# Output projection by seven half-size products, the second half of the tokens tile by tile

## The chip, the cores and the metric

The kernel runs on one core of one Trainium2 chip. The metric is the device time of one execution in microseconds (us). The engines are TensorE (PE in the profile; PEld is its weight load), VectorE (DVE), ScalarE (ACT), GpSimd (POOL) and SyncE (SP), whose queue here only starts DMA transfers.

## The reference, cut to what matters

The input is 1024 tokens of 1024 features in float32. Two attention branches with 512 features each, `y_a` and `y_b`, are merged by gates, projected and added to the input; a SwiGLU feed-forward block follows.

```python
def mixer_block(h, ...):
    proj = h @ w_in                       # 1024 x 4352
    ...
    merged = sigmoid(ga) * (y_a @ w_ba) + sigmoid(gb) * (y_b @ w_bb)    # 1024 x 1024
    return merged @ w_o                   # the output projection, 1024 x 1024 x 1024

h = h + mixer_block(rms_norm(h, norm_mix), ...)
h = h + (silu(hn @ w_gate) * (hn @ w_up)) @ w_down      # hn = rms_norm(h, norm_ffn), 2816 wide
out = rms_norm(h, norm_final)
```

## The kernel before, in words

Every float32 operand of a large product is split in two parts that TensorE takes at full rate: ScalarE writes the high part (line 112), and VectorE or GpSimd subtracts it from the source for the low part (line 113). `split(hi, lo, src, engine)` is this pair; its last argument says who does the subtraction. A product then takes three matmuls for each 128x128 block of weights and 512 columns: high by high, high by low, low by high. Twelve matmuls of 128x512 are a contraction over 512, and are called one step below.

The stages on TensorE, with the start of each in the profiled execution:

- Projections, the windowed attention and the differential attention, with the gate products as filler (to 635.9 us).
- The branch products (`ppa`, line 551, from 635.9). First `y_b @ w_bb`, then `y_a @ w_ba`: 16 steps each, one for every block of 128 features (o) and half of the tokens. For each step VectorE multiplies the sigmoid gate by the PSUM bank (lines 833 and 854). For the second branch GpSimd then adds the first branch's part, which waits in `tb` (line 855), and the sum is split into `mT` (line 856, subtraction on VectorE). The second branch's weight splits (`wbha`) have their subtraction on GpSimd. In the second half of this stage `prep_wo` splits the first blocks of `w_o`, on GpSimd too.
- The output projection (`po`, line 882, from 725.6). For each column half q and group of four token tiles, eight contraction blocks c are accumulated in four PSUM banks; the last column half of the last four tiles goes tile by tile. That is 2 x 8 x 8 x 3 = 384 matmuls. VectorE adds the banks to the input `h2` (`out_add`, line 887). As each token tile is complete, `norm_f` normalises it (ScalarE square, GpSimd root, VectorE scaling, line 1017), and `turn_f` transposes it on TensorE, eight transposes a tile (`ptn_f`, line 1031), into the blocks `b11`, `b21`, `b22` of the feed-forward block's right side, and into the sums of blocks that its products need.
- The gate and up products (`pg`, line 1116, from 818.9). They already go by seven half-size products instead of eight (Strassen's method in Winograd's form): for each of 11 pairs of feature blocks (fp) and both weights (i), products 1, 2, 6, 5, 7, 3, 4 are one step each. Products 1 and 2 need only the blocks themselves; 6, 5, 7 and 4 need sums of token blocks (`t_ops`, split by `split_t`) and sums of weight blocks (lines 940 to 946, on VectorE). The order starts with products 1 and 2 of the first `N_EARLY = 3` pairs, twelve steps that give the other engines time to make the sums.
- The down product (`pd`, line 1210, from 1240.9), by seven products too, and the final normalisation.

PSUM has eight banks of 128x512. Operands live in rings: eight `op` tiles of split weights, five `raw` tiles of loaded ones; a tile is written again when its last reader is done. From the branch products on, the order of TensorE's instructions is the order in which the code writes them; up to the down product, the order on the other engines and on SP's queue is fixed when the program is built, by a planner that simulates the whole. In the chip's queues every instruction waits in place, so what stands behind a waiting instruction on its engine waits too.

```python
    def split(hi, lo, src, lo_eng):                                # lines 111 to 113
        nc.scalar.activation(hi, src, AF.Copy)
        lo_eng.tensor_tensor(lo, src, f32(hi), ALU.subtract)
    ...
        nc.vector.tensor_tensor(gt, gt, ps, ALU.mult)              # lines 854 to 858
        nc.gpsimd.tensor_tensor(gt, gt, tb[:, o, tk], ALU.add)
        split(mT[:, o, 0, tk], mT[:, o, 1, tk], gt, nc.vector)
        if n >= 8:
            prep_wo(0, n - 8)
    ...
        for n, (a, b) in enumerate(((0, 0), (0, 1), (1, 0))):      # lines 881 to 883
            nc.tensor.matmul(ps, mT[:, c, a, t * P:(t + 1) * P], wos[q, c][:, b],
                             start=(c == 0 and n == 0), stop=(c == DC - 1 and n == 2))
```

## Time and profile before

| | us |
|---|---|
| median of 3 runs (lowest, highest) | 1462.27 (1459.82, 1462.70) |
| the profiled execution | 1461.45 |
| its span, first to last instruction | 1459.6 |
| TensorE busy in the span | 1441.7 |
| VectorE, ScalarE, GpSimd busy | 856.9, 660.8, 522.4 |

The span is 1.85 us shorter than the profiled execution's own time; what lies around it is not in the trace. All durations below are from that one execution. The granted TensorE clock is full in it but for the start and the end.

### The profile page before, as it was taken

The page shows a single profiled execution, that of the slowest core. Times are in us where ns is not written, and L with a number is a line of the kernel's source. Part 1 is how long each engine was busy: PE and PEld are TensorE (multiplying, and loading weights), DVE is VectorE, ACT ScalarE, POOL GpSimd, SP SyncE. Part 2 cuts the span into 40 slices and gives each one's busy share as a digit, 9 for nine tenths or more (in the row PEclk, how much of TensorE's full clock was granted, in tenths as well). Part 3 has the DMA queues.
Part 4 walks back from the last instruction along what each step waited for, and adds up shares of the span by engine and source line. Part 5 has one row for each costly group of instructions (what it writes and reads, how often), then busy time and mean ns, then how long its engine had stood idle before and what let it go on. Part 6 is the DMA issues. An engine that isn't in the chain of part 4 may idle for free.

```text
span 1459.6 us, 21074 instructions
## 1 busy us (share of the span) xinstructions
PE 1441.7 (99%) x7375; PEld 1237.3 (85%) x7375; DVE 856.9 (59%) x1680; ACT 660.8 (45%) x1247; POOL 522.4 (36%) x496
## 2 busy tenths in 40 slices
PE   8999999999999999999999999999999999999997
PEld 7998989988898989888788878888888888788886
DVE  6456326528686868433514876555555553787667
ACT  6356336525455555444515643333333333444454
POOL 4143223313323232224834246454444542000444
PEclk9999999999999999999999999999999999999999
DMA  7334453372524251086523534333333333954443
GB/s 238 88 100 114 116 130 90 77 223 84 146 74 145 74 153 66 30 280 205 188 99 128 160 96 152 123 104 99 100 102 109 102 101 102 348 189 140 123 128 139
DMA packets 157241, 192.06 MB, mean 132 GB/s; under 512 B 16256, under 2 KB 101696, under 8 KB 157136
## 3 DMA queue, kind: packets, MB, share of 16 engines
q1 hardware_dynamic: 157136, 190.73, 41.7%
q8 instruction: 58, 0.95, 0.3%
q14 instruction: 47, 0.39, 0.1%
HBM read 130.19 MB, written 53.94 MB: 126 GB/s over the span
## 4 chain that ended last, share of the span: by engine, by line
PE 85%; POOL 4%; issue 4%; DMA 3%; DVE 1%; ACT 1%; SPq 0%; POOLq 0%; ACTq 0%; DVEq 0%
PE pg L1116 28%; PE pp_g L200 11%; PE pd L1210 8%; PE po L882 6%; PE aps L607 4%; PE pp_qb L200 3%; PE pp_va L200 3%; PE pp_ka L200 3%; PE apy L649 3%; PE pp_qa L200 3%; POOL oa L113 3%; PE apt L636 2%; PE ppa L551 2%; PE bpt L338 2%; PE bpy L344 2%
## 5 line engine op out<-in xcount | busy, mean ns | idle before, releaser
L1116 PE MATMUL pg<-t,wop 128*128 128x512 f32 x1056 | 243.1, 389 | 1.6 <-DVE wop L113 1.6
L1116 PEld LDWEIGHTS pg<-t,wop 128*128 128x128 f32 x1056 | 198.1, 188 | 43.3 <-DVE wop L113 2.0
L113 POOL TENSOR_TENSOR wop<-wf,wop 128x512 fp32r<-128x512 f32 x118 | 157.7, 1338 | 156.8 <-ACT wop L112 144.4
L1210 PE MATMUL pd<-ob,oa 128*128 128x512 f32 x924 | 210.2, 389 | 1.6 <-DVE ob L113 1.2
L1210 PEld LDWEIGHTS pd<-ob,oa 128*128 128x128 f32 x924 | 173.3, 188 | 38.5 <-DVE ob L113 1.6
L1116 PE MATMUL pg<-b,wop 128*128 128x512 f32 x792 | 183.2, 389 | 0.0
L1116 PEld LDWEIGHTS pg<-b,wop 128*128 128x128 f32 x792 | 148.5, 188 | 30.7
L113 POOL TENSOR_TENSOR wl_c<-w_c,wh_c 128x1024 fp32r<-128x1024 f32 x32 | 77.6, 2426 | 162.5 <-ACT wh_c L112 130.6
L112 ACT ACTIVATE wop<-wf 128x512 fp32r<-128x512 f32 x128 | 80.2, 631 | 81.9 <-PE pg L1116 50.8
L618 ACT ACTIVATE as<-as,amn 128x1040 f32<-128x1040 f32 x64 | 74.5, 1164 | 73.9 <-DVE amn L613 73.6
L113 POOL TENSOR_TENSOR oa<-ra,oa 128x512 fp32r<-128x512 f32 x33 | 44.0, 1335 | 171.6 <-ACT oa L112 170.2
L200 PE MATMUL pp_g<-hT_hi,wh_c 128*128 128x512 f32 x256 | 101.3, 396 | 0.0
L200 PE MATMUL pp_g<-hT_hi,wl_c 128*128 128x512 f32 x256 | 100.9, 394 | 0.0
L200 PE MATMUL pp_g<-hT_lo,wh_c 128*128 128x512 f32 x256 | 100.9, 394 | 0.0
L112 ACT ACTIVATE oa<-ra 128x512 fp32r<-128x512 f32 x77 | 48.7, 632 | 106.9 <-PE pd L1210 51.8
L607 PE MATMUL aps<-ak,aq 128*128 128x352 f32 (+1 forms) x384 | 92.9, 326 | 0.7 <-DMA ak<-ka_d 0.7
L882 PE MATMUL po<-woh,mT 128*128 128x512 f32 x384 | 88.6, 390 | 0.0
L940 DVE TENSOR_TENSOR s<-wf,wf 128x512 f32<-128x512 f32 x22 | 26.1, 1190 | 105.7 <-DMA wf<-in_w_ff_gate_dram 49.4
L882 PEld LDWEIGHTS po<-woh,mT 128*128 128x128 f32 x384 | 71.7, 188 | 14.7
L607 PEld LDWEIGHTS aps<-ak,aq 128*128 128x128 f32 x384 | 69.6, 188 | 15.1 <-DMA ak<-ka_d 1.0
L613 DVE CUSTOM_DVE_ANT_0 as<-aps,dist,amn 128x352 f32<-128x352 f32 (+1 forms) x128 | 71.3, 563 | 10.1 <-PE aps L607 8.1
L325 POOL TENSOR_SCALAR bs<-bs,bdn 128x432 f32<-128x432 f32 (+1 forms) x64 | 37.0, 596 | 86.9 <-DVE bdn L323 64.7
(258 smaller groups left out, 2951.8 us busy)
## 6 DMA issues: line engine op xcount, KB each, us to landing
ra<-aop SPq DMA_DIRECT2D x77, 256.0 KB, 2.6
w_c<-in_w_in_dram SPq DMA_DIRECT2D x33, 512.0 KB, 4.1
wf<-in_w_ff_gate_dram SPq DMA_DIRECT2D x24, 512.0 KB, 3.8
wf<-in_w_ff_up_dram SPq DMA_DIRECT2D x24, 512.0 KB, 3.8
aop<-as SPq DMA_DIRECT2D x44, 256.0 KB, 2.1
aop<-c SPq DMA_DIRECT2D x33, 256.0 KB, 2.0
g_d<-gate_stage SPq DMA_DIRECT2D x32, 256.0 KB, 2.0
gt<-g_d SPq DMA_DIRECT2D x32, 256.0 KB, 3.4
```

What stands on the lines that cost most here:

```text
L112: nc.scalar.activation(hi, src, AF.Copy)
L113: lo_eng.tensor_tensor(lo, src, f32(hi), ALU.subtract)
L200: nc.tensor.matmul(ps[:, :n], a[:, c, :], b[:, c, at:at + n], start=(c == 0 and i == 0), stop=(c == DC - 1 and i == 2))
L325: nc.gpsimd.tensor_scalar(st[:, r, :W], st[:, r, :W], dn[:, r:r + 1], 1.0, ALU.mult, ALU.mult)
L338: nc.tensor.transpose(pt[:kp, r, :], st[:, r, o:o + P] if k < 8 else md[:, r], ident)
L607: nc.tensor.matmul(ps[:, :n], qs[m][:, t * P:(t + 1) * P], ks[m][:, vv, k0:k0 + n], start=(vv == 0), stop=(vv == 1))
L613: nc.vector.tensor_tensor_reduce(s[m][:, a:b], ps[:, a - k0:b - k0], far_by, slope, low, ALU.add, ALU.min, mn[:, m, i + j:i + j + 1])
L618: nc.scalar.activation(s[m][:, 0:L], s[m][:, 0:L], AF.Exp, bias=low, scale=-1.0, accum_out=dn[:, m:m + 1])
L649: nc.tensor.matmul(py[:, cols], v[:kp, a, k, :], at_[:kp, k, b, :], start=(k == 0 and j == 0), stop=(k == 8))
L882: nc.tensor.matmul(ps, mT[:, c, a, t * P:(t + 1) * P], wos[q, c][:, b], start=(c == 0 and n == 0), stop=(c == DC - 1 and n == 2))
L1116: nc.tensor.matmul(ps, op[:, x, c, :], b[:, y, c, :], start=(p in (1, 2, 5) and c == 0 and n == 0), stop=(p in (4, 2, 3) and c == 3 and n ...
L1210: nc.tensor.matmul(ps[u], oa[:, a, u * P:(u + 1) * P], ob[:, b, :], start=(p in (1, 2, 5) and j == 0 and k == 0), stop=(p in (2, 3, 4) and ...
```

## The change

The output projection, too, goes by seven half-size products. The merged tensor is kept as float32 in four blocks, by half of the features (contraction) and half of the tokens: `a11`, `a12` (first half of the tokens), `a21`, `a22` (second half); `w_o` is loaded in four blocks `w11`, `w21`, `w12`, `w22`. Sums of each are made by VectorE, and by GpSimd for `a21 - a11` and for `w21`. Products 1, 2, 6, 5, 3 are done in steps by contraction block j, for four token tiles u at once; products 7 and 4, which only the second half of the tokens needs, tile by tile (`product_t`), with the transposes of finished tiles between them. `out_add` is called for the banks of every product. `m2` takes the place of `ya0`, the first half of `y_a`; `ahead` makes the splits of the step eight steps later. With this go smaller edits:

- the splits of `w_ba` have their subtraction on VectorE instead of GpSimd; `mT` and its splits are gone, and products 1 and 2 have their eight splits of each side made during the branch products;
- in the feed-forward block products 1 and 2 of a fourth pair come ahead of the sums (`N_EARLY = 4`, 16 steps). The first three pairs keep their product 1 in a PSUM bank as before; the fourth's is copied to SBUF, and ScalarE copies it back into a bank before product 6 adds to it;
- the weight sums of the first pair go to GpSimd; the splits of the token sums are spread over steps 2 to 11; the tiles' transposes come one later.

```diff
-WB_BUFS = 5
+WB_BUFS = 7
-P_BUFS = 7
+P_BUFS = 10
...
+    a21, a22 = (keep.tile([P, 4, 512], F32, name=f"m_{n}") for n in ("21", "22"))
+    m0, m1, ya0 = block_pair(0, "m0", F32), block_pair(1, "m1", F32), block_pair(2, "ya0", F32R)
+    a11, asum, a12, w11 = m0[:, 0], m0[:, 1], m1[:, 0], m1[:, 1]
...
+    def right_o(p, j):
...
+        split(ob[:, 0], ob[:, 1], src, nc.vector)
+    def left_o(p, j):
+        oa = lefts[p, j] = op_tile(f"oa_o{p}_{j}")
+        split(oa[:, 0], oa[:, 1], {1: a11, 2: a12, 6: a11, 5: asum, 3: a12}[p][:, j], nc.gpsimd)
...
+    order_a = [(o, 0) for o in range(6)] + [(0, 1), (6, 0), (1, 1), (7, 0)] + [(o, 1) for o in range(2, DC)]
     for n, (o, half) in enumerate(order_a):
         if o not in ws_a:
-            ws_a[o] = branch_w(ypool, o, w_ba, "a")
+            ws_a[o] = branch_w(ypool, o, w_ba, "a", None, nc.vector)
         gt, ps, tk = gated(1, o, half, ws_a[o], ya)
         nc.vector.tensor_tensor(gt, gt, ps, ALU.mult)
-        nc.gpsimd.tensor_tensor(gt, gt, tb[:, o, tk], ALU.add)
-        split(mT[:, o, 0, tk], mT[:, o, 1, tk], gt, nc.vector)
-        if n >= 8:
-            prep_wo(0, n - 8)
+        nc.gpsimd.tensor_tensor(merged(o, half), gt, merged(o, half), ALU.add)
+        if n < 4:
+            right_o(1, n)
+        elif n < 8:
+            right_o(2, n - 4)
+            left_o(1, n - 4)
+        elif n < 12:
+            if n > 9:
+                left_o(2, n - 10)
+        elif n < 14:
+            left_o(2, n - 10)
+            if n == 12:
+                m2 = block_pair(2, "m2", F32)
+                w22, w12 = m2[:, 0], m2[:, 1]
+                load_wo(w12, 0, 1)
+                load_wo(w22, 1, 1)
...
+    for j in range(4):
+        tt_v(asum[:, j], a21[:, j], a22[:, j], ALU.add)
+        tt_p(a21[:, j], a11[:, j], a21[:, j], ALU.subtract)
+        tt_v(a11[:, j], asum[:, j], a11[:, j], ALU.subtract)
+        tt_v(w11[:, j], w12[:, j], w11[:, j], ALU.subtract)
+        tt_v(t2[j // 2][:, j % 2 * 512:j % 2 * 512 + 512], w22[:, j], w11[:, j], ALU.subtract)
+    steps_o = [(p, j) for p in (1, 2, 6, 5, 3) for j in range(4)]
...
+    for n, (p, j) in enumerate(steps_o):
...
+        for u in range(4):
+            for k in (2, 3) if last else (j,):
+                product_o(p, k, u)
+            if j == 3:
+                out_add(u + 4 * (p == 5), int(p > 2), sets_o[p][u])
+                if p == 3:
+                    norm_f(u)
+        for k in (n - 1, n) if last else (n,):
+            ahead(k)
+            if k < 4:
+                tt_v(a12[:, k], a12[:, k], a11[:, k], ALU.subtract)
+            elif k < 8:
+                tt_p(w21[:, k - 4], w21[:, k - 4], t2[(k - 4) // 2][:, k % 2 * 512:k % 2 * 512 + 512], ALU.subtract)
+            elif k < 12:
+                tt_v(w12[:, k - 8], w22[:, k - 8], w12[:, k - 8], ALU.subtract)
+    TURN_O = {1: 0, 2: 1, 3: 2, 4: 3, 6: 4}
+    for n, (p, u) in enumerate(((7, 0), (7, 1), (4, 0), (4, 1), (7, 2), (7, 3), (4, 2), (4, 3))):
+        product_t(p, u)
+        out_add(4 + u, int(p == 7), set1[u])
+        if p == 4:
+            norm_f(4 + u)
+        if n in TURN_O:
+            turn_f(TURN_O[n])
...
-    N_EARLY = 3
+    N_EARLY, N_KEPT = 4, 3
-        tt = nc.vector.tensor_tensor
+        tt = nc.vector.tensor_tensor if fp else nc.gpsimd.tensor_tensor
...
+        late = N_KEPT <= fp < N_EARLY
+        if p in (1, 2, 5) or (late and p == 6):
             u[which] = ps_bank(f"pg_{nm}_{p}")
+        if late and p == 6:
+            nc.scalar.copy(ps, u[1])
-    TURN, SPLIT = {0: 6, 2: 7}, {0: (0, 1), 1: (2,), 3: (3,)}
+    TURN = {0: 5, 2: 6, 4: 7}
+    SPLIT = {2: (0, (6, 5)), 3: (1, (6, 5)), 5: (2, (6, 5)), 7: (3, (6, 5))} | {8 + u: (u, (7, 4)) for u in range(4)}
```

## The prediction

> **What bounds the kernel now.** I read the page first (engines, clock), then the waits of TensorE, then the chain that ended last, and then stretches and groups around the output projection.

> ```profile
> span 1459.6 us, 21074 instructions
> PE 1441.7 (99%) x7375; PEld 1237.3 (85%) x7375; DVE 856.9 (59%) x1680; ACT 660.8 (45%) x1247; POOL 522.4 (36%) x496
> PEclk9999999999999999999999999999999999999999
> ```

> TensorE is busy in all but 18 us at the full granted clock. So a matmul less shortens the run by its whole interval, provided the others keep up; and a wait of TensorE lengthens it by its whole length. The waits of TensorE (line, whom for, us in total, times, longest):

> ```profile
> PE ppa L551 <- POOL wbha L113: 1.7, 1, 1.7
> PE pg L1116 <- DVE wop L113: 1.6, 1, 1.6
> PE pd L1210 <- DVE ob L113: 1.2, 1, 1.2
> ```

> Two of the three lie around the change: one in the second branch product, for a split on GpSimd, one where the first pair's sums begin. The chain gives the pace (start, us, matmuls):

> ```profile
> 725.80 51.68 PE po L882 x228
> 777.49 0.87 PE ptn_f L1031 x8
> 789.24 21.81 PE po L882 x96
> 817.38 1.75 PE ptn_f L1031 x16
> 854.90 386.14 PE pg L1116 x1702
> ```

> 386.14 / 1702 = 0.227 us a matmul; a step of twelve is 2.72, a tile's eight transposes 0.87. Output projection and transposes have no gap between 725.8 and 818.9.

> **The change part by part.** The profiled execution took 1461.45 us, 1.85 more than its span and 0.8 less than the median, 1462.27.

> *Matmuls.* Seven products in place of eight: 20 + 8 steps, 336 matmuls instead of 384. 48 x 0.227 = **10.9 us off**. Transposes, branch products and everything from the first feature product on keep their counts. The edit of the fourth pair moves steps forward and adds none.

> *The wait in the branch product (1.7).* This is GpSimd's stage:

> ```profile
> 700.00:720.00 20.00, 18.34 (x82) 14.85 (x81) 11.59 (x14) 9.45 (x16) 18.62 (x13) 1.00 0.58 183
> 820.00:840.00 20.00, 20.00 (x94) 16.64 (x93) 20.00 (x33) 16.34 (x30) 0.81 (x3) 1.00 0.81 219
> 840.00:860.00 20.00, 18.39 (x81) 14.69 (x80) 14.98 (x25) 9.45 (x17) 6.30 (x4) 1.00 0.22 67
> ```

> (stretch, length, then busy us of PE, PEld, DVE, ACT, POOL.) From 700 to 720 GpSimd was busy 18.6 of 20 us. The change takes the eight `wbha` splits from it, and swaps eight `w_o` splits for eight left splits. VectorE gets those eight and eight right splits for the sixteen of `mT`; six of the `wbha` splits stand ahead of the stage in its order, and the last stands ahead of the eighth step's multiply, while the tenth step is the first to read it. **1.7 off.** If VectorE should be late with one, it is by a fraction of a step, as PSUM's eight banks let TensorE run ahead.

> *The wait where the sums begin (1.6).* From 820 to 840 VectorE was busy throughout, and product 6 of the first pair waited at 854.9 for a split behind its sums. Now 16 steps stand ahead of it, not 12 (10.9 us more cover), and the eight weight sums are on GpSimd, which had 0.8 us of work there. **1.6 off.** The eight sums and the four last early splits on GpSimd can begin when step 4 frees an operand tile; 12 x 1.3 us = 16 against 11 steps (30 us). The extra copies are two of ScalarE in a stage where it has half its time free: nothing.

> *What comes onto the path: product 6 of the output projection.* Its left side needs all of `a21 + a22`, and its right side `w12` and `w22`, which lie where `ya0` was, so that their loads wait until TensorE is done with the tenth step of the second branch (call that T). TensorE then has six steps of that branch and eight of products 1 and 2, and reaches product 6 at T + 14 x 2.72 = T + 38.1; bank u = 3 of it, after nine more matmuls, at T + 40.1. By the order of the changed program VectorE must have done by then, from the first sum with `w12` to the fourth addition of product 1 to `h2` (which frees that bank): 24 sums and 3 right splits, with two SBUF inputs each, and 5 multiplies and 4 additions that read PSUM. What these cost:

> ```profile
> L113 DVE TENSOR_TENSOR mT<-gt,mT 128x512 fp32r<-128x512 f32 x16 | 15.7, 979 | 19.0 <-ACT mT L112 18.8
> L854 DVE TENSOR_TENSOR gt<-gt,ppa 128x512 f32<-128x512 f32 x16 | 10.7, 677 | 1.3 <-ACT gt L822 1.3
> L1017 DVE SCALAR_TENSOR_TENSOR xn_f<-h,rstd_f,gffn 128x1024 f32<-128x1024 f32 x8 | 10.7, 1341 | 6.6 <-POOL rstd_f L118 6.6
> 853.56 0.68 DVE L946 TENSOR_TENSOR wf<-wf,wf 128x512 f32<-128x512 f32 x1
> 854.16 1.28 DVE L113 TENSOR_TENSOR wop<-wf,wop 128x512 fp32r<-128x512 f32 x2
> 863.52 1.73 DVE L940 TENSOR_TENSOR s<-wf,wf 128x512 f32<-128x512 f32 x1 [7.47 <-POOL wop L113]
> 853.70 4.75 POOL L113 TENSOR_TENSOR wop<-s,wop 128x512 fp32r<-128x512 f32 x2 [32.73 <-DVE p L1131]
> 858.42 7.99 POOL L113 TENSOR_TENSOR wop<-wf,wop 128x512 fp32r<-128x512 f32 x6
> av<-va_d SPq DMA_DIRECT2D x4, 1024.0 KB, 5.3
> h<-in_x_dram SPq DMA_DIRECT2D x8, 512.0 KB, 6.2
> ```

> Undisturbed, operations of VectorE start 0.60 apart (853.56 to 854.16), GpSimd's take 7.99 / 6 = 1.33. A load of 1024 KB lands after 5.3, so VectorE begins at T + 5.3 and needs 36 x 0.60 = 21.6: done at T + 26.9, with 13 us to spare. But operations with two SBUF inputs and GpSimd's hold each other up: the sum at 863.52 took 1.73 while GpSimd worked, and at 853.70 two of GpSimd's took 4.75 instead of 2.66 while VectorE worked. The multiplies that read PSUM show nothing of it (677 on average in GpSimd's busiest stage). In this stretch GpSimd does 5 gate additions, 8 of the sums and 2 left splits, 15 x 1.33 = 20 us. If each held up VectorE for its full length, the fourth addition would end at T + 46.9, 6.8 late; if none did, it would be in time. Besides, the chain is not free to run through: `a21 + a22` waits for GpSimd's gate additions, `a11`'s sum for GpSimd's `a21`. Going through the two orders operation by operation with these durations, letting whoever asks first go first, I get the second and fourth additions late, by 1.8 and 0.5, and all splits in time. I take **2.5 us on**, between 0 and 6.8. The loads of `h2` (6.2) start as the last gate addition ends, near T + 28, and are in time for it.

> [...]

> *The later products.* After product 6 a step of 2.72 needs one right split (0.60, 1.7 held up), one bank addition (0.6) and one left split (1.33): it fits. At the first tile of product 4 TensorE must wait until product 7's bank is added, and that addition stands in VectorE's queue behind the scaling of `xn_f` (1.34): about 0.5 late, from 0 to 1.5. **0.5 on.** The transposes find their `xn_f` five us early. Twelve more bank additions (12 x 0.6) are beside TensorE.

> *The wait at the down product (1.2)* stays: the order of the loads there is as before.

> Sum: -10.9 - 1.7 - 1.6 + 2.5 + 0.5 = **-11.2 us**. From the profiled execution that is 1450.2, from the median 1451.1; I take **1450.5**.

> **The rivals.**

> 1. *VectorE waits for all of GpSimd's work ahead of product 6* (6.8 instead of 2.5), and 1.5 at product 4: -14.2 + 8.3 = -5.9, 1456. For it: the rows at 863.52 and 704 to 720 (979 on average for `mT`). Against: at 853.70 it was GpSimd that waited. 0.15.

> 2. *The same, with the loads late.* `w12` and `w22` are asked for together with gate loads. The slowest group of loads,

> ```profile
> ak<-ka_d SPq DMA_DIRECT2D x16, 260.0 KB, 9.1
> ```

> took 9.1: 3.8 more on the chain. -5.9 + 3.8 = -2.1, 1460, not to be told from before. 0.07.

> 3. *Slower: VectorE's operations all stand still while GpSimd works, those on PSUM too.* Then the two engines are one queue from T + 5.3 to the first feature product. VectorE has in it 36 + 17 splits + 24 additions + 10 transposes' parts, 87 x 0.60, and 8 x 1.34, together 63; GpSimd 33 + 4 operations, 37 x 1.33 = 49, and sixteen small ones of 0.57,

> ```profile
> L117 POOL TENSOR_SCALAR rstd_f<-ss_f 128x1 f32<-128x1 f32 x8 | 4.7, 585 | 34.8 <-ACT xn_f L1015 34.5
> L118 POOL TENSOR_TENSOR rstd_f<-rstd_f,neg_half 128x1 f32<-128x1 f32 x8 | 4.4, 552 | 0.7
> ```

> 9: 121 us. TensorE's own work there is 6 steps less 5.3, 28 steps and six tiles' transposes: 11.0 + 76.2 + 5.2 = 92.4. It decides once the sum passes 92.4; in full it costs 29: -14.2 + 29, 1476. Without VectorE's 43 operations that read PSUM it is 26 less and comes to 95, about what TensorE needs. Against it: the 677 of L854. 0.1 for this and whatever else would put over 3 us net on the path.

> 4. *No new wait at all:* -14.2, 1447.5. 0.18; the forecast's side.

> **How the numbers follow.** The forecast (a net 9 to 13 off) has 0.5, no new wait 0.18, the first rival 0.15, the second 0.07, slower 0.1. The range starts at no new wait from the lowest of the runs (1459.8 - 14.2 = 1445.6; 1446) and takes in the first rival with 3 us for a late load: 1459. What a measurement can tell from no change is about 0.2%, 2.9 us: below 1459.3 faster, above 1465.2 slower. Faster 0.82, same 0.07, slower 0.11.

> **What would show it.** Right: 336 matmuls of `po`; no wait of `ppa` for `wbha` and none of `pg` at the first pair's product 6; a wait of `po` for VectorE of 1 to 4 us, some 38 us after the tenth step, and one under 1.5 among the tiles. Wrong: a wait of `po` of over 10 us for either engine; `pg` waiting for GpSimd's sums; the split at the start of the first branch product late, now that `yb` comes in eight loads; or a pace that isn't 0.227.

## The result, and the profile after

The change makes the kernel slightly slower, by 0.2%. Its median is 1463.2 us (1460.7 to 1466.6, 22 runs) against 1459.7 (22 runs of the kernel before beside them): a ratio of 1.0020, 95% interval 1.0011 to 1.0029. The forecast was 1450.5, with a range up to 1459.

The page of the profiled execution of after, in the lines that answer to the first ones shown of before:

```profile
span 1460.8 us, 21057 instructions
PE 1435.5 (98%) x7327; PEld 1230.6 (84%) x7327; DVE 925.3 (63%) x1724; ACT 673.4 (46%) x1267; POOL 553.2 (38%) x512
PEclk9999999999999999999999999999999999999999
```

The 48 matmuls are gone (7327 for 7375), yet TensorE is busy only 6 us less, where 48 x 0.227 is 10.9; and the span is 1.2 us longer. So the time lies in two places: in waits, and in matmuls that run slower. First the waits of TensorE (line, whom for, us in total, times, longest; rows of the stages after 600 us):

```profile
PE po L1108 <- DVE h L921: 3.9, 2, 2.5
PE pg L1200 <- ACT ts L1084: 3.3, 1, 3.3
PE pg L1200 <- DVE c L1210: 1.8, 2, 1.1
PE po L1116 <- DVE h L921: 1.2, 1, 1.2
PE pd L1294 <- DVE ob L113: 1.1, 1, 1.1
PE ppa L551 <- DVE wbha L113: 0.3, 1, 0.3
```

Of the two waits that were to go one is gone, and of the other 0.3 us are left, now for VectorE. (A second wait of 0.3 in this stage, for GpSimd, is for a weight split of the first branch.) In their place stand 3.9 us ahead of product 6 of the output projection, 5.1 in the early feature steps, and 1.2 at the first tile of product 4. The row that names ScalarE is VectorE's too: the copy `ts` (line 1084) that gives the PSUM bank back stands in ScalarE's queue behind the high part of a split of `kept`, which waits for VectorE's sum at 845.31 (further down):

```profile
846.02 0.63 ACT L112 ACTIVATE t<-kept 128x512 fp32r<-128x512 f32 x1 [3.97 <-DVE kept L1082]
846.62 0.59 ACT L1084 COPY ts<-ptn_f 128x512 f32<-128x512 f32 x1
```

The page's line of the clock, in 40 slices of 36.5 us, shows only nines. Finer stretches (stretch, length, busy us of PE, PEld, DVE, ACT and POOL, granted clock, DMA share, GB/s) show what it hides:

```profile
745.35:748.76 3.41, 0.93 (x3) 0.48 (x3) 3.38 (x5) 1.15 (x2) 1.28 (x1) 1.00 0.31 125
748.76:752.17 3.41, 2.34 (x6) 1.82 (x6) 3.41 (x5) 2.90 (x6) 2.19 (x2) 0.50 0.00 0
752.17:755.58 3.41, 3.41 (x9) 2.48 (x8) 3.41 (x4) 3.04 (x6) 3.41 (x3) 0.50 0.00 0
844.33:847.74 3.41, 0.48 (x2) 0.44 (x3) 3.41 (x4) 1.72 (x4) 3.41 (x4) 1.00 0.46 150
847.74:851.16 3.42, 3.42 (x10) 2.64 (x9) 3.42 (x4) 1.52 (x3) 3.42 (x4) 0.50 0.02 6
```

After each of the two long waits the granted clock is 0.50, for 6.83 and for 3.41 us. TensorE's matmuls start 0.427 us apart in that time (0.227 at 1.00). Taken as half pace, that is (2.34 + 3.41) / 2 = 2.9 us lost after the first, 3.42 / 2 = 1.7 after the second; by the two intervals it is 2.7 and 1.6.

The account: -10.9 (matmuls) - 1.3 (branch products) + 3.9 + 2.9 (product 6 and its half clock) + 1.2 (tiles) + 5.1 - 1.6 + 1.7 (early feature steps and their half clock) = +1.0, against a span that is 1.2 longer. That it comes so close is partly chance. Ahead of the branch products, where TensorE's work is the same, this execution happens to be 1.15 us shorter than that of before; and the output projection and the feature products together take some 1.5 us more than these terms, which is not placed.

Why VectorE is late shows where it works beside GpSimd. VectorE, then GpSimd, then the first of TensorE's two waits, ahead of product 6 (start, us, what, [idle before]):

```profile
740.17 1.78 DVE L1096 TENSOR_TENSOR m<-m 128x512 f32<-128x512 f32 x1
741.87 1.78 DVE L113 TENSOR_TENSOR ob_o<-t,ob_o 128x512 fp32r<-128x512 f32 x1
743.58 1.77 DVE L1146 TENSOR_TENSOR m<-m,m 128x512 f32<-128x512 f32 x1
745.27 0.68 DVE L1096 TENSOR_TENSOR m<-m 128x512 f32<-128x512 f32 x1
...
746.59 0.68 DVE L921 TENSOR_TENSOR h<-h,po 128x512 f32<-128x512 f32 x1
...
739.66 1.74 POOL L113 TENSOR_TENSOR oa_o<-m,oa_o 128x512 fp32r<-128x512 f32 x1
741.36 1.75 POOL L1095 TENSOR_TENSOR m<-m,m 128x512 f32<-128x512 f32 x1
743.06 1.74 POOL L113 TENSOR_TENSOR oa_o<-m,oa_o 128x512 fp32r<-128x512 f32 x1
...
747.42 0.93 PE L1108 MATMUL po<-ob_o,oa_o 128*128 128x512 f32 x3 [2.46 <-DVE h L921]
```

From 740.17 to 745.27 the two take turns: one operation of each every 1.70 us, where VectorE's alone start 0.60 apart (738.75 to 739.35 in experiment 2) and GpSimd's shortest `oa_o` takes 1.28. An operation of GpSimd costs VectorE, which has a backlog, 1.10 us here, nearly twice the 0.60 that it would take to do that operation itself. The same is seen in the early feature steps, where GpSimd has the first pair's eight weight sums (lines 974 to 980) and eight early splits. Four of these splits, the third pair's, were on VectorE in the kernel before: the last argument of that `split` changed from `0 < fp < N_EARLY` to `fp == 1`, an edit that the list of smaller edits does not name. The other four are the fourth pair's.

```profile
841.93 3.46 DVE L113 TENSOR_TENSOR t<-kept,t 128x512 fp32r<-128x512 f32 x2
845.31 0.68 DVE L1082 TENSOR_TENSOR kept<-ptn_f,kept 128x512 f32<-128x512 f32 x1
845.91 0.67 DVE L1083 TENSOR_TENSOR kept<-kept,ptn_f 128x512 f32<-128x512 f32 x1
846.51 1.79 DVE L113 TENSOR_TENSOR t<-ts,t 128x512 fp32r<-128x512 f32 x1
...
841.42 1.74 POOL L975 TENSOR_TENSOR wf<-wf 128x512 f32<-128x512 f32 x1
843.13 1.71 POOL L113 TENSOR_TENSOR wop<-wf,wop 128x512 fp32r<-128x512 f32 x1
844.80 1.72 POOL L974 TENSOR_TENSOR s<-wf,wf 128x512 f32<-128x512 f32 x1
```

The two operations with a PSUM operand (845.31, 845.91) take 0.68 and 0.67, beside one of GpSimd's (844.80, 1.72 long); they are late only because they stand behind the others. Over whole stretches (columns as above, for the three that were shown of before):

```profile
700.00:720.00 20.00, 19.69 (x87) 16.00 (x86) 11.54 (x13) 7.48 (x12) 16.09 (x12) 1.00 0.55 197
820.00:840.00 20.00, 19.90 (x92) 16.07 (x90) 19.33 (x24) 18.11 (x34) 11.39 (x7) 1.00 0.75 208
840.00:860.00 20.00, 14.92 (x57) 11.26 (x56) 19.27 (x18) 8.19 (x15) 16.51 (x12) 0.91 0.20 67
```

From 820 to 840 VectorE was full before and is full now, but gets through 24 operations instead of 33, as GpSimd went from 0.8 to 11.4 us of work. From 840 to 860 GpSimd went from 6.3 to 16.5, and VectorE from 15.0 to 19.3, though it executes seven operations fewer there (18 for 25). (The feature products start 5.65 us earlier in after, so the stretches answer to each other only roughly.)

### The profile page after: what moved, and what is told of

It reads as the page before. It is cut to its first block, busy times and chain, and to the rows that moved or that the text cites. A ratio compares the mean times of both kernels' runs of the same rounds, so it can differ in the third digit from the quotient of the medians.

```text
span 1460.8 us, 21057 instructions
## 1 busy us (share of the span) xinstructions
PE 1435.5 (98%) x7327; PEld 1230.6 (84%) x7327; DVE 925.3 (63%) x1724; ACT 673.4 (46%) x1267; POOL 553.2 (38%) x512
## 3 DMA queue, kind: packets, MB, share of 16 engines
q1 hardware_dynamic: 158512, 189.68, 40.6%
## 4 chain that ended last, share of the span: by engine, by line
PE 82%; DVE 6%; issue 4%; POOL 4%; DMA 2%; ACT 1%; SPq 1%; POOLq 0%; DVEq 0%; ACTq 0%
PE pg L1200 26%; PE pp_g L200 11%; PE pd L1294 8%; PE aps L607 4%; PE apy L649 3%; PE pp_va L200 3%; PE pp_ka L200 3%; PE pp_qb L200 3%; PE pp_qa L200 3%; POOL oa L113 3%; PE po L1108 2%; PE ppa L551 2%; PE apt L636 2%; PE bpt L338 2%; PE bpy L344 2%
## 5 line engine op out<-in xcount | busy, mean ns | idle before, releaser
L113 POOL TENSOR_TENSOR wop<-wf,wop 128x512 fp32r<-128x512 f32 x122 | 165.7, 1360 | 172.6 <-ACT wop L112 161.7
L1200 PE MATMUL pg<-b,wop 128*128 128x512 f32 x792 | 186.2, 393 | 5.2 <-ACT ts L1084 3.3
L113 POOL TENSOR_TENSOR wl_c<-w_c,wh_c 128x1024 fp32r<-128x1024 f32 x32 | 77.7, 2427 | 162.5 <-ACT wh_c L112 138.3
L112 ACT ACTIVATE wop<-wf 128x512 fp32r<-128x512 f32 x128 | 80.5, 633 | 79.8 <-PE pg L1200 53.9
L113 POOL TENSOR_TENSOR oa<-ra,oa 128x512 fp32r<-128x512 f32 x33 | 44.1, 1336 | 171.4 <-ACT oa L112 170.0
L112 ACT ACTIVATE oa<-ra 128x512 fp32r<-128x512 f32 x77 | 48.6, 632 | 107.8 <-PE pd L1294 52.7
L974 DVE TENSOR_TENSOR s<-wf,wf 128x512 f32<-128x512 f32 x20 | 18.3, 916 | 96.7 <-DMA wf<-in_w_ff_up_dram 53.3
L613 DVE CUSTOM_DVE_ANT_0 as<-aps,dist,amn 128x352 f32<-128x352 f32 (+1 forms) x128 | 71.2, 563 | 10.2 <-PE aps L607 8.1
L621 POOL TENSOR_SCALAR as<-as,adn,neglam 128x1040 f32<-128x1040 f32 x32 | 39.0, 1219 | 75.2 <-DVE adn L619 75.2
L315 DVE CUSTOM_DVE_ANT_0 bs<-bps,tbx,nsink 128x432 f32<-128x432 f32 (+1 forms) x64 | 38.4, 624 | 41.6 <-PE bps L313 38.5
## 6 DMA issues: line engine op xcount, KB each, us to landing
w_c<-in_w_in_dram SPq DMA_DIRECT2D x33, 512.0 KB, 4.1
wf<-in_w_ff_gate_dram SPq DMA_DIRECT2D x25, 512.0 KB, 3.6
wf<-in_w_ff_up_dram SPq DMA_DIRECT2D x25, 512.0 KB, 3.6
```

Source lines behind the costliest of these rows:

```text
L315: nc.vector.tensor_tensor_reduce(st[:, r, :W], ps[:, :W], tb, 2.0 ** -(4 * g + r + 1), nsink[:, 4 * g + r:4 * g + r + 1], ALU.add, ALU.min ...
L613: nc.vector.tensor_tensor_reduce(s[m][:, a:b], ps[:, a - k0:b - k0], far_by, slope, low, ALU.add, ALU.min, mn[:, m, i + j:i + j + 1])
L621: (nc.gpsimd if t % 4 in COMBINE_POOL else nc.vector).tensor_scalar(s[1][:, 0:L], s[1][:, 0:L], dn[:, 1:2], neglam, ALU.mult, ALU.mult)
L1200: nc.tensor.matmul(ps, op[:, x, c, :], b[:, y, c, :], start=(p in (1, 2, 5) and c == 0 and n == 0), stop=(p in (4, 2, 3) and c == 3 and n ...
```

## The experiments

Theory 1: GpSimd's operations hold VectorE up, so work given to GpSimd costs VectorE more than it takes off. Theory 2: VectorE simply has too much to do, and GpSimd's share relieves it. Theory 3: the early waits come from the fourth pair, its PSUM banks and ScalarE's copies. In the table "po" is the time from the first matmul of the output projection to the first of the gate and up products, "pg" from there to the first of the down product, in the profiled execution. Half clock (us at 0.50) leaves out the start and the end of the program, where before and after have some too (3.41 us each within the first 20 us, 2.99 and 2.07 at the end). Experiment 8 is a test of the clock and stands apart.

| kernel | median | ratio to before (95%) | po | pg | half clock |
|---|---|---|---|---|---|
| before | 1459.7 | | 93.25 | 421.97 | 0 |
| after | 1463.2 | 1.0020 (1.0011, 1.0029) | 90.20 | 428.88 | 10.2 |
| 1: pair 0's sums on VectorE | 1459.3 | 0.9994 (0.9980, 1.0007) | 89.21 | 426.76 | 6.8 |
| 2: the output projection's sums on VectorE | 1456.8 | 0.9980 (0.9968, 0.9991) | 83.60 | 428.80 | 3.4 |
| 3: both | 1454.2 | 0.9957 (0.9941, 0.9973) | 83.69 | 426.97 | 3.4 |
| 4: after with three early pairs | 1463.8 | 1.0027 (1.0016, 1.0038) | 89.49 | 429.81 | 13.7 |
| 5: both, early splits on VectorE | 1450.1 | 0.9939 (0.9924, 0.9953) | 83.63 | 421.84 | 0 |
| 6: as 5, order of the tiles | 1448.5 | 0.9918 (0.9905, 0.9931) | 82.34 | 422.73 | 0 |
| 7: as 2, idle work on GpSimd | 1466.3 | 1.0046 (1.0029, 1.0064) | 94.98 | 428.85 | 17.1 |
| 9: as 6, three early pairs | 1450.5 | 0.9944 (0.9929, 0.9959) | 82.20 | 423.71 | 0 |
| 10: as 6, w_ba splits on GpSimd | 1451.4 | 0.9946 (0.9934, 0.9958) | 83.58 | 422.74 | 0 |

(Before is 1459.7 beside 1 to 4, 1460.5 beside 5 to 8, 1459.5 beside 9 and 10. Number 3's profiled execution, 1459.5, is the longest of its ten runs, with a wait of 2.1 us in the attention and 3.41 us at half clock behind it, which the table leaves out: its stage lengths stand, its span doesn't. Medians and ratios of different groups differ by up to 1 us for the same kernel before, so between those groups the stage lengths are the finer measure.)

**1. The first pair's weight sums back on VectorE.**

```diff
-        tt = nc.vector.tensor_tensor if fp else nc.gpsimd.tensor_tensor
+        tt = nc.vector.tensor_tensor
```

> Only the weight sums of the first feature pair (eight operations) go back from GpSimd to VectorE; all else as in the kernel after. Theory 1 (held up): in the trace of after VectorE's operations on SBUF start 1.70 apart while GpSimd works, against 0.60 alone, so each of GpSimd's operations costs a VectorE that has a backlog 1.10, more than the 0.60 of doing the sum itself. 8 x 0.5 = 4 us less for VectorE by 855 us; the three waits in the early steps (5.1 us) shrink to about 1, and the 1.7 us lost to the half clock after the longest go: 1463.2 - 5.8 = 1457.4 (1456 to 1459.5). Theory 2 (too much work): VectorE has too many operations there, and GpSimd's share relieves it: 8 x 0.6 = 4.8 us more, waits of 10, 1468. Theory 3 (fourth pair): the waits come from the fourth pair's steps and ScalarE's extra copies: no change, 1463.

4.0 us faster than after, of the 5.8 expected; but only 2.1 of it is in the feature stage. Another 1.0 is in the output projection, which the edit leaves alone: TensorE waits 4.0 us there as in after, but 3.4 us at half clock follow instead of 6.83, which the edit doesn't explain. Theories 2 and 3 are out for these sums: eight operations more on VectorE, and TensorE waits less. But 3.4 us of wait (5.1 in after) and 3.41 at half clock remain in the early steps; the eight early splits on GpSimd (experiment 5) are the rest.

**2. The output projection's sums on VectorE.**

```diff
-    tt_v, tt_p = nc.vector.tensor_tensor, nc.gpsimd.tensor_tensor
+    tt_v, tt_p = nc.vector.tensor_tensor, nc.vector.tensor_tensor
```

> Only the eight sums of the output projection that GpSimd does (a21 and w21) go to VectorE. Theory 1: 8 x (1.10 - 0.60) = 4 us less for VectorE before product 6's fourth bank; of the two waits there (3.9 us) at most 1 is left, and the 3.4 us lost to the half clock after them (6.83 us at 0.50) go: 1463.2 - 6.5 = 1456.7 (1455.5 to 1458.5). The early feature steps keep their 5.1 us. Theory 2: 8 x 0.6 = 4.8 us more, waits of 8.7 and a longer half clock: 1468 to 1471. A third (the loads of h2 or of the two blocks of w_o are what is late): no change, 1463.

6.4 us faster than after, where 6.5 was expected; the output projection is 6.6 shorter and the feature stage the same. The wait ahead of product 6 and its half clock are gone. VectorE in this run, with eight operations more to do:

```profile
738.75 0.68 DVE L1096 TENSOR_TENSOR m<-m 128x512 f32<-128x512 f32 x1
739.35 0.68 DVE L1095 TENSOR_TENSOR m<-m,m 128x512 f32<-128x512 f32 x1
739.96 0.68 DVE L1096 TENSOR_TENSOR m<-m 128x512 f32<-128x512 f32 x1
740.56 0.67 DVE L921 TENSOR_TENSOR h<-h,po 128x512 f32<-128x512 f32 x1
```

Its first bank addition (line 921) starts at 740.56, in after it was 746.59. Late loads are out as a cause: none was moved.

**3. Both edits.**

> Both edits: all sixteen sums on VectorE. Theory 1: the two gains add: 1463.2 - 5.8 - 6.5 = 1451 (1449 to 1455), faster than the kernel before (1459.7). Theory 2: 1473 or more. Theory 3 for the early steps with theory 1 for product 6: 1457.

1454.2, 9.0 us under after and 5.5 under before, where 12.3 under after was expected; the two gains nearly add (4.0 + 6.4 = 10.4). The feature stage is as long as in experiment 1: what the forecast missed is there again.

**4. Three pairs ahead of the sums instead of four.**

```diff
-    N_EARLY, N_KEPT = 4, 3
+    N_EARLY, N_KEPT = 3, 3
```

> Only the fourth pair ahead of the sums is undone (three pairs, twelve steps, no extra copies of a fourth pair); the first pair's sums stay on GpSimd. Theory 1: the fourth pair is not the cause; VectorE has the same work with four steps (10.9 us) less of cover, so the waits of the early steps stay at 5 us or grow, up to 16: 1463 to 1474. Theory 3: the waits there (5.1) and the half clock behind the longest (1.7) go, and the first pair's 1.6 may come back: 1456.4 to 1458.

1463.8: theory 3 is out. Without the fourth pair and its copies the waits of the early steps come to 5.7 us, of which one alone is 5.0, with 6.83 us at half clock behind it.

**5. The early splits on VectorE as well.**

```diff
-split(op[:, 0], op[:, 1], src, nc.vector if (p in first and fp == 1) or ...
+split(op[:, 0], op[:, 1], src, nc.vector if (p in first and 0 < fp < N_EARLY) or ...
```

> The sixteen sums on VectorE as in the run before this, and also the subtractions of the eight splits for products 1 and 2 of the third and fourth pair, which the change had given to GpSimd. In the trace with the sixteen sums on VectorE those eight take 1.75 each on GpSimd from 828 to 843 us, VectorE's operations on SBUF there start 1.70 apart, and TensorE still waits 0.2 + 0.7 + 2.7 us, with 3.41 us at half clock after. Theory 1 (held up): VectorE gains 8 x 0.5 = 4 us; the three waits and the 1.7 us of half clock go: 1454.2 - 5 = 1449.2 (1448 to 1451). Theory 2 (VectorE has too many operations): 8 x 0.6 = 4.8 us more work for it, waits of 8 us: 1459 to 1461. Theory 3 (banks and ScalarE's copies): 1454.

1450.1, 4.1 us under experiment 3, with 5 expected. The two ratios' intervals overlap, so it is the stage that shows it: the feature stage is 5.1 shorter, and as long as before the change. These are the stretches that answer to 820 to 860 of after (the stage starts 7.25 us earlier here), columns as above:

```profile
813.00:833.00 20.00, 20.00 (x94) 16.62 (x93) 19.34 (x33) 19.27 (x37) 0.00 (x0) 1.00 0.73 204
833.00:853.00 20.00, 19.59 (x86) 15.54 (x85) 15.55 (x27) 9.48 (x18) 6.80 (x5) 1.00 0.26 85
```

GpSimd does nothing from 813 to 833, and VectorE, as full as in after, gets through 33 operations in 20 us where it did 24.

**6. A third step between a tile's bank addition and the next use of the bank.**

```diff
-((7, 0), (7, 1), (4, 0), (4, 1), (7, 2), (7, 3), (4, 2), (4, 3))
+((7, 0), (7, 1), (7, 2), (4, 0), (4, 1), (7, 3), (4, 2), (4, 3))
```

> The kernel with the sixteen sums and the eight early splits on VectorE, and the second half's tiles in the order 7.0, 7.1, 7.2, 4.0, 4.1, 7.3, 4.2, 4.3 (product.tile) instead of 7.0, 7.1, 4.0, 4.1, 7.2, 7.3, 4.2, 4.3, so that a third step stands between a tile's bank addition and the product that needs the bank again. If the 1.2 us wait there is the bank addition standing behind the scaling of xn_f, it goes: 1.2 us under the kernel with the old order, 1448. If it is the whole of VectorE that is late there, the wait moves to the next tile: no change, 1449.2.

1448.5 against 1450.1 beside it, 1.5 less, though the two intervals overlap. The output projection is 1.3 shorter, and the wait of 1.2 us at line 1116 is gone; but the feature stage is 0.9 longer, 0.7 of it a wait for `p` (line 1216) that was 0.4 and is 1.1. So both halves of the expectation have a part, and by the stages the edit is worth 0.4 us. It has the lowest median of the kernels: 0.9918 of before. TensorE's remaining waits in the stages of the change, from its list of waits:

```profile
PE pg L1200 <- DVE p L1216: 1.1, 1, 1.1
PE ppa L551 <- DVE wbha L113: 0.3, 1, 0.3
PE po L1108 <- DVE h L921: 0.3, 1, 0.3
```

**7. Work on GpSimd that nobody waits for.** It is the kernel of experiment 2, with sixteen operations that read `w22`, which lies still until long after.

```diff
+    extra = late_pool.tile([P, 256], F32, name="extra")
+    for j in range(16):
+        h = j % 2 * 256
+        nc.gpsimd.tensor_tensor(extra, w22[:, j // 2 % 4, h:h + 256], gffn[:, h:h + 256], ALU.add)
```

> The kernel whose eight sums of the output projection are on VectorE (1456.8 us; no wait ahead of product 6, its last bank addition ends 0.4 us ahead of need, its first 3.2), plus sixteen operations of GpSimd on 128x256 that read SBUF and that nobody waits for, spread by the planned order over the stretch in which VectorE makes its sums (716 to 750 us). VectorE's own instructions and their order stay the same. Theory 1 (held up): each holds VectorE up by about half of 1.10 us, 8 us in all; product 6 waits 4 to 6 us for VectorE's bank additions, and 1.7 to 3.4 us of half clock follow: 1463 to 1466. Rival (the wait came from the dependence on GpSimd's result, a21): nobody depends on these, so no change but a left split that is late behind them, at most 1 to 2 us: 1457 to 1459.

9.5 us slower than experiment 2, and the output projection 11.4 longer. VectorE, and GpSimd beside it:

```profile
726.66 3.51 DVE L1153 TENSOR_TENSOR w<-w,t 128x512 f32<-128x512 f32 x3
748.18 0.67 DVE L921 TENSOR_TENSOR h<-h,po 128x512 f32<-128x512 f32 x1
...
722.72 6.91 POOL L1103 TENSOR_TENSOR extra<-m,gffn 128x256 f32<-128x256 f32 x6
```

GpSimd's operations on half as many columns come at 6.91 / 6 = 1.15 each, and VectorE's, on 512 columns, at 3.51 / 3 = 1.17; the first bank addition is at 748.18 instead of 740.56, 7.6 us later where 8 was worked out. Nothing that VectorE does depends on these sixteen, and its list shows no idle time from 716 to 752, so the dependence on `a21` is out as the cause. TensorE waits 6.5 us there (4.4 for a left split whose sum is late on VectorE, 2.1 for bank additions), and the clock is at half for 13.65 us. TensorE works for 9.8 of these, so at half pace 4.9 are lost.

**8. Waits put in by hand.** In the kernel before, twelve steps of the feature products wait for a chain of operations that begins at the end of the step before.

```diff
+        if (fp, p, i) in stalls:
+            hi = op[:, 0]
+            nc.vector.scalar_tensor_tensor(hi, four(last_ps[0]), 0.0, f32(hi), ALU.mult, ALU.add)
+            for _ in range(stalls[fp, p, i]):
+                nc.scalar.activation(hi, f32(hi), AF.Copy)
```

> The kernel before, with twelve waits put into the feature products by hand, 24.5 us apart: TensorE waits at the end of a step for one operation of VectorE on its bank and then 0, 3, 1, 4, 2 or 5 copies of ScalarE (0.63 each), twice through, so some 1.2, 3.1, 1.9, 3.7, 2.5 and 4.4 us. It measures what a wait costs beyond its length. Theory A: the granted clock halves in whole windows of 3.41 us after every wait of about 2.4 us or more, as in the traces of after (a wait of 2.5 with one of 1.5 behind it: 6.83 us at 0.50; one of 3.3: 3.41 us), each window costing 1.7 us: 33.6 us of waits and 14 to 20 us of half clock, 1507 to 1513. Theory B: only a wait as long as a whole window does it, the two longest kinds: 4 x 1.7 = 7, 1500. Theory C: a wait costs its length alone and the half clock in after had another cause: 1493.

1517.7 us, in a single run. The span grew by 56.3 us; 39.0 are the waits themselves, and 34.1 us were at half clock, which at half pace costs 17.1 and explains nearly all of the rest. Theory C is out, and so is B: a wait of 2.06 us was enough. But theory A's 2.4 us isn't the rule either, since waits of 2.73 and 2.98 us cost nothing more. In before and after all changes of the granted clock lie a multiple of 3.413 us apart (in after the fall at 748.76, the rise at 755.58, the fall at 847.74 and the rise at 851.16: 2, 27 and 1 times 3.413), and what separates the rows below is how much of one such window TensorE idles (same columns; windows in pairs around the waits that end at 961.14, 990.47, 1050.30 and 1224.17):

```profile
956.29:959.70 3.41, 0.79 (x4) 0.33 (x2) 1.89 (x3) 1.68 (x3) 1.90 (x2) 1.00 0.69 232
959.70:963.11 3.41, 1.97 (x5) 1.58 (x6) 1.08 (x2) 1.32 (x3) 0.00 (x0) 0.50 0.04 12
987.01:990.42 3.41, 1.40 (x7) 0.82 (x5) 0.69 (x1) 1.74 (x3) 1.97 (x2) 1.00 0.33 85
990.42:993.83 3.41, 3.36 (x8) 2.69 (x9) 1.39 (x2) 0.00 (x0) 0.48 (x1) 0.50 0.72 236
1045.03:1048.44 3.41, 2.54 (x12) 1.77 (x10) 0.21 (x1) 1.81 (x4) 1.28 (x1) 1.00 0.21 78
1048.44:1051.86 3.42, 1.56 (x7) 1.28 (x8) 1.36 (x3) 1.54 (x3) 1.26 (x1) 1.00 0.66 185
1219.11:1222.52 3.41, 2.08 (x10) 1.38 (x8) 3.33 (x5) 1.35 (x3) 2.30 (x2) 1.00 0.50 154
1222.52:1225.94 3.42, 1.77 (x8) 1.47 (x9) 1.28 (x2) 1.26 (x2) 0.74 (x1) 1.00 0.20 77
```

A window with 1.40 us of work was followed by half clock (in experiment 7 one with 1.43, from 849.69), one with 1.56 was not, nor were two of before with 1.75 and 1.80 (from 709.14 and 852.50). The 2.06 us wait lay within one window but for its last 0.05; those of 2.73 and 2.98 fell across a boundary. After a window at half clock with 1.97 us of work, with 2.34 in after and with 3.03 in experiment 7 (from 754.12) the window behind stayed at 0.50; after one with 3.36 the clock was full again. No limit between 1.43 and 1.56 is shown beyond these stages of 128x512 matmuls: in the first 20 us of the program, with transposes and matmuls of 256 columns, windows with 1.73 us of work (before) and 1.78 (after) were followed by half clock too. Why is open.

**9. Three early pairs in the best kernel.** The edit of experiment 4, in the kernel of experiment 6.

> The kernel with the sixteen sums and the eight early splits on VectorE and the new order of the tiles (1448.5), without the fourth pair ahead of the sums: twelve steps of cover, as in the kernel before, where product 6 of the first pair waited 1.6 us. If the fourth pair does its part, TensorE waits there again: VectorE was busy throughout to 845 us with sixteen steps, so with four steps (10.9 us) less, but four splits and the copies less too (about 4 us), it is 2 to 6 us late: 1450.5 to 1456, with a half clock where it passes 2 us. If VectorE undisturbed needs no more than twelve steps: 1448.5. If the fourth pair's own steps cost something (its copies, its banks): 1447.

1450.5, the low end of what was expected if the fourth pair does its part. The feature stage is 1.0 us longer (waits of 0.7 + 0.6 + 0.6 us against one of 1.1). The two intervals just meet, so the fourth pair is worth about 1 us by the stages, and no more is shown.

**10. The `w_ba` splits back on GpSimd, in the best kernel.**

```diff
-            ws_a[o] = branch_w(ypool, o, w_ba, "a", None, nc.vector)
+            ws_a[o] = branch_w(ypool, o, w_ba, "a")
```

> The same 1448.5 kernel, with the subtractions of the eight splits of w_ba back on GpSimd, as in the kernel before. If the edit was worth what the forecast gave it, the branch product waits 1.7 us for GpSimd again and nothing else happens: 1450.2. Theory 1 (GpSimd holds VectorE up) adds that the splits take the place of VectorE's time between 680 and 720 us, where it is busy 65 to 82% with them itself; product 6 has 0.4 us of slack, so a wait of 1 to 3 us can come back there: 1450 to 1454. If TensorE runs ahead of both: 1448.5.

1451.4. The stages show 0.6 us in the second branch product, where the wait for GpSimd is 0.6, and 1.2 in the output projection, where product 6 waits 1.2 for VectorE's additions instead of 0.3: both parts of the expectation, the first at a third of its 1.7 us, the second at its low end. The other 1.1 us of the difference in medians is not placed. (The 1451.4 and the 1448.5 were taken beside different runs of before; by the ratios the difference is clear.)

## Why the prediction was wrong, point by point

Three steps failed: the half clock was not in the sum, the hold-up of VectorE by GpSimd was left out in the first feature steps, and it was taken too small ahead of product 6.

**The matmuls (-10.9): right.** 336 of `po`, and 0.227 apart where the clock is full (0.44 ns for each of 512 columns; the float32 transposes, whose operands aren't split, take 0.87 / 8 = 0.109 us, 0.85 ns for each of 128). Experiment 6 has the output projection 10.9 us shorter than before; 0.9 of that is one tile's transposes that moved to the feature stage, and 0.3 of wait is left in it, so 10.3 are the matmuls'.

**The wait in the branch product (-1.7): right,** -1.3 measured (the waits of the branch products went from 1.9 to 0.6 us in all). By experiment 10 the edit was worth more, in the kernel of experiment 6, through VectorE's additions (1.2 us) than through the wait that it removed (0.6).

**Product 6 (+2.5, from 0 to 6.8): right mechanism, mis-sized.** It waited 3.9, for VectorE's additions as described. The step that failed is the walk through the two orders, "letting whoever asks first go first". It had the fourth addition 0.5 late, at T + 40.6, so that VectorE's 36 operations took 13.7 us more than their own 21.6. The trace has the same 36 operations without a pause from 712.86 to 752.40, 39.5 us, so that they lost 17.9. GpSimd began 19 operations in that stretch, where I had counted 15, and from 740.17 to 745.27 the two engines go strictly in turn, 1.70 for each pair. The first addition came at 746.59, when TensorE had been waiting since 744.96. How far the walk went wrong by the count and how far by the turns is not known. Experiment 7 shows the turns with work that nothing depends on (1.15 for each of GpSimd's, 1.17 for each of VectorE's). The first rival took 6.8 here, which is what the wait and its half clock came to (3.9 + 2.9). That is luck: it had no half clock in it, and its wait was further off than the 2.5.

**The half clock: a missing term,** 2.9 us here and 1.7 in the early steps, 4.6 in all. "A wait of TensorE lengthens it by its whole length" was the sentence that failed: where a window held some 2 us or more of idle time (2.01 to 2.93 in the rows above with half clock behind them), each window of 3.41 us at half clock behind it cost up to 1.7 us more. No wait of before was long enough to show it, outside the program's start and end: its emptiest window there still holds 1.75 us of work. The 98.99 us between the falls at 748.76 and 847.74 are 29.0 times 3.413. The length of a wait alone doesn't decide it: in experiment 8 2.06 us did it and 2.98 did not.

**The first feature steps (-1.6): the largest miss.** The old wait went, as forecast. But I costed the work moved to GpSimd from GpSimd's side alone ("12 x 1.3 us = 16 against 11 steps") and never charged VectorE for it, in the very stretch where the profile of before had it busy throughout. I priced that hold-up in the next paragraph, for product 6. The count was short too: besides the eight sums GpSimd does eight early splits here, not four, and the sixteen last from 828.6 to 854.5. Measured: 5.1 us of new wait and 1.7 of half clock, 6.8 that the forecast had at nothing, of the 12.4 us between forecast and measured span. Experiments 1 and 5 take it back, and the stage is then as long as before.

**ScalarE's copies (nothing): right,** by experiment 4.

**The tiles (+0.5, up to 1.5): right mechanism, 1.2 measured;** experiment 6 removes it.

**The rivals.** That all of VectorE's operations stand still, those on PSUM too, did not happen: the additions to `h2` took 0.67 to 0.69 in after, and 0.67 in the rows of experiments 2 and 7. Late loads played hardly a part: the block that VectorE waited for came 5.8 us after it was asked for, where I took 5.3. The true course, the known hold-up in a second place plus the clock, was none of the five.

How good was the sum without the hold-up? Experiment 5 is the change with GpSimd's work out of VectorE's way and the tiles in the order of the change. From the branch products to the end it is 12.0 us shorter than before in the profiled executions (8.9 us by the ratio of all runs, 0.9939). My sum without product 6's 2.5 is -13.7. So the gains were somewhat overrated, and that the forecast -11.2 lies near this kernel's time is chance, as it holds 2.5 for a hold-up that this kernel doesn't have.

## What to carry to other kernels

Where VectorE had a backlog, an operation moved from it to GpSimd cost it more (1.10 us) than doing it (0.60); both read two operands from SBUF here. So move work to GpSimd in stretches where VectorE has time to spare, and charge every stretch of GpSimd's work to both engines. Look at the granted clock in stretches of a few us around each wait of TensorE of about 2 us or more (2.06 was enough here), and around shorter ones close behind (1.47 in after): the page's slices of 36.5 us hid it, and each window of 3.41 us at half clock added up to 1.7 us to the wait.
